# Norms in steps, a first norm by tokens, weight halves at the start, and gate tiles made while the pooling is awaited

## The chip, the cores and the metric

The kernel runs on one core of one Trainium2 chip. Its engines each have their own instruction stream: PE (TensorE, matrix products, with its weight loads PEld), DVE (VectorE), ACT (ScalarE), POOL (GpSimd) and SP (SyncE), which here issues the transfers from memory. They wait for each other by semaphores. The metric is the device time of one execution in microseconds (us); less is better.

## The reference

The kernel computes a network of two layers over 256 latent tokens and 256 context tokens (together 512 columns, the two "streams"), model width 1024. What is computed, cut to what matters:

```python
for l in range(DEPTH):                       # DEPTH = 2
    mod = (silu(c) @ w_ada[l] + b_ada[l])    # 9 vectors of 1024: shifts, scales, gates; one set per stream
    h  = ffn_half_step(h, ...)               # h + 0.5 * gate * ((silu(u @ w1) * (u @ w3)) @ w2)
    hc = ffn_half_step(hc, ...)              #   with u = rmsnorm(h) * g * (1 + scale) + shift
    y, yc = token_mixer(u, uc, ...)          # u, uc: normed and modulated again
    h = h + mod[:, :, 5] * y
    h = ffn_half_step(h, ...)                # second half step; context too, but not in the last layer

def token_mixer(u, uc, ...):
    cq, ckv, kr, pz, gq, gk, gv, ga, gr, gates = split_cols(u @ w_in)
    o_a = blocked_attend(q, k_all, v_all)    # 8 heads; low-rank q, k, v with norms and rotary
    o_p = multiscale_pool(pz, w_pool, pool_scale)
    og  = gla_bidir(qg, kg, vg, log_a, s_f, s_b)    # gated linear attention, two scans, chunks of 64
    o_g = rmsnorm(og) * silu(gr)
    g = sigmoid(gates)                       # three gates of 1024 columns
    m = g[0] * (o_a @ w_branch[0]) + g[1] * (o_p @ w_branch[1]) + g[2] * (o_g @ w_branch[2])
    return m @ w_out
```

All of it is in float32 accuracy.

## The kernel before, in words

**Products.** Activations lie with features on the partitions, tokens in the columns. A weight tile is loaded as `raw`, split by ACT into a rounded part `whi` (line 185) and by DVE into the rest `wlo = raw - whi` (`split`, line 197). An activation is split in the same way (`uhi`/`ulo`, `hi`/`lo`). `mm3` (lines 215 to 221) makes one product of three matmuls: hi·whi (L219), lo·whi (L220), hi·wlo (L221). Nearly all of PE's time is such triples.

**Weights and slots.** `Weights.run_ahead` (line 94) issues loads in the order of use while fewer than RAWS = 4 raw tiles are held, and splits them while the number of held parts stays under `room`. All SBUF tiles of 128x512 come from one pool of NSLOT = 71 slots (`slot`), given out in the order in which the program asks.

**Order of the work.** The program is written out by Python; each engine runs its instructions in the order in which a scheduler puts them, near the order of the text. Two helpers mix work into places where PE would wait: `ada` makes the modulation vectors in units (`adas(n)` advances them, DVE multiplies into `adaacc`, line 358, or PE makes them with `ada` matmuls, line 327), and `filler` (line 750) makes the mixer's later column tiles.

**Start** (`setup`, line 234; `setup_rest`, line 291). SP issues the first weight tile, the eight tiles of x and context, then the `ada` tiles of column groups j = 0, 2 (sixteen of 256 KB), three more raw tiles, groups 1 and 3. PE transposes x (line 283) into `h`; the squares and their sum `acc` (`square`, lines 440 to 448) go over features, so `ms` (line 464, a product of `acc` with a constant that sums over the partitions) and `rstd` are ready only after all of `h`. Then `am`, the scale vectors, and the first norm's `ut` (471), `uhi` and `ulo` (475). `dense_first` (line 520) takes units of both w1 and w3 over the full contraction, in parts by stream.

**A norm** (`norm`, line 455) is a generator that makes both streams' `ms`, `rstd`, `uhi` and `ulo` in one step, when the next stage begins. `grow` (line 493) adds a finished tile to `h` (line 501), squares it and adds it to `acc` (line 448). A stage ends with the second stream of its last tiles; PE then makes `ms` for both streams. The transitions stand, by the profile's time, at 422 (feed-forward to mixer), 899 (mixer to feed-forward), 1277 (feed-forward to feed-forward of the next layer), 1646 (feed-forward to mixer) and 1949 (mixer to the last feed-forward, one stream).

**Mixer** (`mixer`, line 665). Attention (`attend`, line 866) and the linear attention (`gla`, line 1133) are generators that yield the name of a step; after each, the pooling branch advances by one and `FILL[l][name]` credits are added; one credit advances the filler by half a column tile (12 matmuls). The filler makes the tiles of the pooling, then, in `while len(self.op) < 4: yield 1`, does nothing until the pooling is ready, then the pooling's branch with its gates, four output gates `gr`, the attention's branch, and the linear attention's branch. Steps that the prediction speaks of: `kms`, sums of squared keys (line 932); `qsum` and `rq`, the same of the queries (988, 1017); `sc`, `p`, `pt`, `pT`, `av`: scores, their exponents, transposes, copies and values (1031 to 1067); `logit`, `la`, `ket`, `A`, `ds`, `st`, `o`, `orstd`, `ot` of the linear attention (1157 to 1264), which runs two scan directions; in layer 1 first a pair for the context, then one for the latents.

## Time and profile before

| | |
|---|---|
| three runs | 2153.69, 2155.99, 2154.8 us; median 2154.8 |
| the profiled run | 2152.27 us, its span 2150.5 us |
| granted clock, mean | 0.983 |
| PE, DVE, ACT busy | 97%, 68%, 41% of the span |
| data moved | 290.43 MB, mean 135 GB/s |

A row of the timeline gives start, length, engine, line, operation, `out<-in`, sizes and a count; in brackets stands how long the engine stood idle before it, and whose end released it. A row of waits gives who waited for whom: total, times, longest. In a window's row stand busy us and counts of PE, PEld, DVE, ACT and POOL, then the granted PE clock as a share of full speed, the share of DMA engines in use and GB/s. The clock is at full or at half speed; a mean between these says for how much of the window it was half.

### The profile page before, as it was taken

The page shows a single profiled execution, that of the slowest core. Times are in us where ns is not written, and L with a number is a line of the kernel's source. Part 1 is how long each engine was busy: PE and PEld are TensorE (multiplying, and loading weights), DVE is VectorE, ACT ScalarE, POOL GpSimd, SP SyncE. Part 2 cuts the span into 40 slices and gives each one's busy share as a digit, 9 for nine tenths or more (in the row PEclk, how much of TensorE's full clock was granted, in tenths as well). Part 3 has the DMA queues.
Part 4 walks back from the last instruction along what each step waited for, and adds up shares of the span by engine and source line. Part 5 has one row for each costly group of instructions (what it writes and reads, how often), then busy time and mean ns, then how long its engine had stood idle before and what let it go on. Part 6 is the DMA issues. An engine that isn't in the chain of part 4 may idle for free.

```text
span 2150.5 us, 29894 instructions
## 1 busy us (share of the span) xinstructions
PE 2084.2 (97%) x11388; PEld 1752.5 (81%) x11388; DVE 1453.7 (68%) x2870; ACT 882.3 (41%) x1797; POOL 2.0 (0%) x10
## 2 busy tenths in 40 slices
PE   7999999898999999999999989999999998999999
PEld 4888778786777887888888888888888777998997
DVE  4577877867586665666876785767544687666564
ACT  5232223455344555433223342323343656665552
POOL 0000000000000000000000000000000000000000
PEclk9999999999999999999999999999999989999999
DMA  9355554514432223445555453546442332566663
GB/s 318 100 152 157 172 166 134 160 39 127 118 108 69 79 69 98 119 124 152 164 164 161 135 149 102 151 141 186 137 115 59 96 101 80 142 163 192 181 197 127
DMA packets 431071, 290.43 MB, mean 135 GB/s; under 512 B 16464, under 2 KB 386768, under 8 KB 430928
## 3 DMA queue, kind: packets, MB, share of 16 engines
q1 hardware_dynamic: 430016, 287.09, 46.6%
q8 instruction: 89, 1.46, 0.3%
q10 hardware_dynamic: 912, 1.44, 0.2%
q14 instruction: 54, 0.44, 0.1%
HBM read 287.44 MB, written 1.05 MB: 134 GB/s over the span
## 4 chain that ended last, share of the span: by engine, by line
PE 74%; DVE 11%; DMA 9%; ACT 3%; issue 2%; ACTq 0%; SPq 0%; DVEq 0%
PE ps L219 17%; PE ps L220 17%; PE ps L221 17%; DMA raw<-in_ffn_w_dram 9%; PE fill L219 4%; PE fill L221 4%; PE fill L220 4%; DVE wlo L197 4%; DVE adaacc L358 2%; ACT whi L185 2%; PE sc L1031 1%; PE av L1067 1%; PE ada L327 1%; PE pt L1049 1%; PE gv L219 1%
## 5 line engine op out<-in xcount | busy, mean ns | idle before, releaser
L197 DVE TENSOR_TENSOR wlo<-raw,whi 128x512 fp32r<-128x512 f32 (+3 forms) x912 | 531.3, 619 | 290.0 <-ACT whi L185 279.6
L185 ACT ACTIVATE whi<-raw 128x512 fp32r<-128x512 f32 (+3 forms) x912 | 471.9, 568 | 521.5 <-DMA raw<-in_ffn_w_dram 469.8
L219 PE MATMUL ps<-uhi,whi 128*128 128x512 f32 (+1 forms) x1620 | 564.3, 350 | 8.7 <-ACT uhi L185 5.1
L221 PE MATMUL ps<-uhi,wlo 128*128 128x512 f32 (+1 forms) x1620 | 561.8, 348 | 1.1 <-DVE wlo L197 1.1
L220 PE MATMUL ps<-ulo,whi 128*128 128x512 f32 (+1 forms) x1620 | 562.3, 348 | 0.0
L219 PEld LDWEIGHTS ps<-uhi,whi 128*128 128x128 f32 x1620 | 308.0, 191 | 53.7 <-ACT uhi L185 8.7
L221 PEld LDWEIGHTS ps<-uhi,wlo 128*128 128x128 f32 x1620 | 308.8, 191 | 41.3 <-DVE wlo L197 3.6
L220 PEld LDWEIGHTS ps<-ulo,whi 128*128 128x128 f32 x1620 | 309.3, 191 | 37.9 <-DVE ulo L475 0.6
L358 DVE SCALAR_TENSOR_TENSOR adaacc<-raw,csil,adaacc 128x512 f32<-128x512 f32 x420 | 294.6, 744 | 1.6 <-DMA raw<-in_w_ada_dram 0.8
L219 PE MATMUL ps<-hi,whi 128*128 128x512 f32 (+1 forms) x738 | 272.8, 371 | 6.9 <-DVE h L501 5.4
L221 PE MATMUL ps<-hi,wlo 128*128 128x512 f32 (+1 forms) x738 | 272.0, 369 | 0.2 <-DVE wlo L197 0.2
L220 PE MATMUL ps<-lo,whi 128*128 128x512 f32 (+1 forms) x738 | 271.5, 368 | 0.0
L219 PE MATMUL fill<-uhi,whi 128*128 128x512 f32 (+1 forms) x576 | 203.9, 354 | 0.0
L221 PE MATMUL fill<-uhi,wlo 128*128 128x512 f32 (+1 forms) x576 | 195.9, 340 | 0.0
L220 PE MATMUL fill<-ulo,whi 128*128 128x512 f32 (+1 forms) x576 | 195.4, 339 | 0.0
L219 PEld LDWEIGHTS ps<-hi,whi 128*128 128x128 f32 x738 | 141.2, 191 | 29.8 <-DVE h L501 5.8
L221 PEld LDWEIGHTS ps<-hi,wlo 128*128 128x128 f32 x738 | 141.2, 191 | 23.2 <-DVE wlo L197 0.6
L220 PEld LDWEIGHTS ps<-lo,whi 128*128 128x128 f32 x738 | 141.3, 192 | 22.4 <-DVE lo L197 0.2
L570 DVE TENSOR_TENSOR silu<-silu,ps 128x512 f32<-128x512 f32 (+1 forms) x88 | 54.2, 616 | 133.7 <-ACT silu L185 79.3
L185 ACT ACTIVATE silu<-ps 128x512 f32<-128x512 f32 (+1 forms) x88 | 47.4, 539 | 195.4 <-PE ps L221 195.1
L219 PEld LDWEIGHTS fill<-uhi,whi 128*128 128x128 f32 x576 | 109.3, 190 | 21.7 <-issue 10.6
L220 PEld LDWEIGHTS fill<-ulo,whi 128*128 128x128 f32 x576 | 109.4, 190 | 13.5 <-issue 2.4
(265 smaller groups left out, 2192.0 us busy)
## 6 DMA issues: line engine op xcount, KB each, us to landing
raw<-in_ffn_w_dram SPq DMA_DIRECT2D x198, 512.0 KB, 4.4
raw<-in_w_ada_dram SPq DMA_DIRECT2D x128, 512.0 KB, 3.8
raw<-in_w_in_dram SPq DMA_DIRECT2D x86, 512.0 KB, 4.4
...
raw<-in_w_branch_dram SPq DMA_DIRECT2D x48, 256.0 KB, 2.9
ada<-in_w_ada_dram SPq DMA_DIRECT2D x32, 256.0 KB, 5.4
...
```

The source lines that it names most:

```text
L185: i = self.nc.scalar.activation(**k)
L197: self.nc.vector.tensor_tensor(out=lo, in0=src, in1=f32hi, op=ALU.subtract)
L219: mm(out, wh, xh, start=start, stop=False)
L220: mm(out, wh, xl, start=False, stop=False)
L221: mm(out, wl, xh, start=False, stop=stop)
L327: nc.tensor.matmul(ps[32 * g:32 * g + 32, :], self.csil[:, k, :], r[i], start=(k < 4), stop=(k >= 4))
L358: nc.vector.scalar_tensor_tensor(out=acc[s], in0=r[i], scalar=c, in1=acc[s], op0=ALU.mult, op1=ALU.add)
L570: nc.vector.tensor_tensor(out=s[:, 0:n], in0=s[:, 0:n], in1=p3[:, 0:n], op=ALU.mult)
L1031: nc.tensor.matmul(sc[:, 0:nk], q[h][:, tt * P:(tt + 1) * P], keys[h][:, k0:T], start=True, stop=True)
L1049: nc.tensor.transpose(pt[:, (2 * x + j) * P:(2 * x + j + 1) * P], ps_[j][:, (kt + x) * P:(kt + x + 1) * P], self.ident)
L1067: nc.tensor.matmul(av[0][64 * x:64 * x + 64, s * NL:(s + 1) * NL], v[2 * s + kt][:, (h + x) * 64:(h + x) * 64 + 64], pts[x][kt // 2][:, (k ...
```

## The change

- **Start.** x is loaded first, the first raw tiles behind the first `ada` groups, and at most three ahead of group 1. ACT squares x by tokens (`xsq`, summing along the row), DVE multiplies x by the token's factor into `xr`, PE transposes `xr` (32 transposes) into `hr`, besides the residual (32 as before, 16 now behind the first `ada` group). `first_norm` makes `uhi` on ACT from `hr` by scale and bias. `both` loads halves of the contraction, of w1 and w3 together; `dense_first` goes over half of the contraction for all six outputs, then over the other. `wlo` of the first tiles is put behind `ulo` (`seconds`). `setup_rest`'s loads go from ACT's queue to SP's.
- **Norms.** `norm` yields after each stream's mean. `norm_ahead` makes the first stream's mean inside the last stage, before its last 33 matmuls (before the last tile of the output product, in the mixer); `norm_go` fetches that stream's `uhi`, and the second stream's mean follows in `dense` after two steps of the first (`then`). `rstd` has a tile of its own.
- **Mixer.** While the pooling is awaited, up to GATES = (2, 12) tiles of `later` (the eight gates of the pooling's branch, then the four output gates) are made. FILL, POOL and two places of `yield` change.

The core of the diff:

```diff
-NHALF, NSLOT, ROOM_FFN, ROOM_MIX, RAWS = 4, 71, 20, 20, 4
-ROOM_0, ROOM_1, LAST = 8, 36, 4
-S0, S1, S2 = 7, 3, 3
-        dict(a0=1, a1=1.5, k=2, q=3.5, qs=0.5, s=2, t=2, g1=0.5, g2=0, g3=0.5, g4=1, g5=0.5, w=0.5))
-POOL = (0, 1)
+NHALF, NSLOT, ROOM_FFN, ROOM_MIX, RAWS = 4, 70, 20, 20, 4
+ROOM_1, ROOM_2, LAST = 16, 36, 4
...
+        dict(a0=1, a1=1.5, k=2, v=0, q=3.5, qs=1.5, s=2, t=2, g1=1.5, g2=0, g3=1, g4=1, g5=0.5, w=0.5))
+POOL = (1, 1)
+GATES = (2, 12)
...
+        second = lambda: self.nc.vector.tensor_tensor(out=lo, in0=src, in1=f32hi, op=ALU.subtract)
+        if self.net.seconds is None:
+            second()
+        else:
+            self.net.seconds.append(second)
...
+    def both(self, srcs, k0, c0):
+        views = [s[k0 * P:(k0 + 4) * P, c0:c0 + P].rearrange("(k p) c -> p k c", p=P) for s in srcs]
+        def load(t):
+            return [self.nc.sync.dma_start(out=t[:, i * T:(i + 1) * T].rearrange("p (k c) -> p k c", k=4), in_=v)
+                    for i, v in enumerate(views)]
+        return self.w.get(load, 2 * T, lambda r, hi, lo: self.halves(r, hi, lo, 2 * T))
...
+                self.w.run_ahead(3)
...
+        sums, fac = self.tiny(8, "xsum"), self.tiny(8, "xfac")
+        junk = self.slot(name="xsq")
+        xr = []
+        for j in range(4):
+            for c in range(2):
+                self.act(out=junk, in_=xin[j][c], func=AF.Square, accum_out=sums[:, 2 * j + c:2 * j + c + 1])
+            f = fac[:, j:j + 1]
+            nc.vector.tensor_tensor(out=f, in0=sums[:, 2 * j:2 * j + 1], in1=sums[:, 2 * j + 1:2 * j + 2], op=ALU.add)
+            self.act(out=f, in_=f, func=AF.Ln, scale=1.0 / D, bias=self.eps[:, 0:1])
+            self.act(out=f, in_=f, func=AF.Exp, scale=-0.5)
+            xr.append([self.slot(name="xr") for _ in range(2)])
+            for c in range(2):
+                normed = nc.vector.tensor_scalar(out=xr[j][c], in0=xin[j][c], scalar1=f, scalar2=None, op0=ALU.mult)
+        self.xin = xin
+        self.residual(range(4), [normed])
+        self.hr = []
         for k in range(KD):
-            ps = self.ps()
-            for j in range(4):
-                nc.tensor.transpose(ps[:, j * P:(j + 1) * P], xin[j][k // 4][:, (k % 4) * P:(k % 4 + 1) * P], self.ident)
+            t = self.slot(name="hr")
             if k % 2:
-                self.act(out=self.h[:, k, :], in_=ps, func=AF.Copy)
+                self.act(out=t, in_=self.turned(xr, k), func=AF.Copy)
             else:
-                nc.vector.tensor_copy(self.h[:, k, :], ps)
-            for s in range(2):
-                self.square(k, s)
+                nc.vector.tensor_copy(t, self.turned(xr, k))
+            self.hr.append(t)
...
-            i = nc.scalar.dma_start(out=to, in_=src)
+            i = nc.sync.dma_start(out=to, in_=src)
             if self.tc:
-                self.behind(i, self.users[-1:])
+                self.behind(i, [self.last])
...
-        if l == 0 and i == 0:
-            for c in streams:
-                mean(c)
+        for s, c in enumerate(streams):
+            mean(c)
             yield u
-            for parts in (([0], range(1, 4)), (range(4, KD),)):
-                for ks in parts:
-                    for s, c in enumerate(streams):
-                        some(s, c, ks)
-                yield
-        else:
-            for s, c in enumerate(streams):
-                mean(c)
-                some(s, c, range(KD))
+            some(s, c, range(KD))
             yield u
+    def norm_ahead(self, l, i):
+        order = [(l, i) for l in range(DEPTH) for i in (0, 3, 6)]
+        self.ahead = self.norm(*order[order.index((l, i)) + 1], T)
+        next(self.ahead)
+    def norm_go(self, l, i, n):
+        norm = self.ahead
+        if norm is None:
+            norm = self.norm(l, i, n)
+            next(norm)
+        self.ahead = None
+        u = next(norm)
+        return u, lambda: [next(norm) for _ in range(2)] if n == T else None
+    def first_norm(self):
+        nc = self.nc
+        u = []
+        for ks in ([0], [1], [2, 3], range(4, KD)):
+            for k in ks:
+                assert {(0, 0, k // 4), (0, 1, k // 4)} <= self.have
+                hi, lo = self.slot(F32R, "uhi"), self.slot(F32R, "ulo")
+                u.append((hi, lo))
+                for s in range(2):
+                    c = slice(s * NL, (s + 1) * NL)
+                    t, a, b = self.half("ut"), self.am[0][1][:, k, s:s + 1], self.mod[0][:, k, s:s + 1]
+                    self.act(out=hi[:, c], in_=self.hr[k][:, c], func=AF.Identity, scale=a, bias=b)
+                    nc.vector.tensor_scalar(out=t, in0=self.hr[k][:, c], scalar1=a, scalar2=b, op0=ALU.mult, op1=ALU.add)
+                    nc.vector.tensor_tensor(out=lo[:, c], in0=t, in1=hi[:, c].bitcast(F32), op=ALU.subtract)
+            yield u
+        self.hr = None
...
-    def dense(self, units, x, n, by_stream=False):
+    def dense(self, units, x, n, by_stream=False, then=None):
         out = [self.ps() for _ in units]
         n = n if isinstance(n, list) else [n] * len(units)
                     c = slice(s * NL, (s + 1) * NL) if by_stream else slice(0, m)
                     if c.stop <= m:
                         self.mm3(o[:, c], unit.block(k), (x[k][0][:, c], x[k][1][:, c]), k == 0, k == nk - 1)
+                if then and s == 0 and k == 1:
+                    then()
...
+        out = [self.ps() for _ in range(6)]
+        for half, groups in ((0, (range(4), range(4, 6))), (1, (range(6),))):
             for g in groups:
-                for cs, ks in ((both, [0]), (streams, [1, 2, 3])) if k0 == 0 else ((streams, [4, 5, 6]), (both, [7])):
-                    for c in cs:
-                        for k in ks:
-                            for j in g:
-                                self.mm3(out[j][:, c], units[j].block(k), (x[k][0][:, c], x[k][1][:, c]), k == 0, k == KD - 1)
-                            if then:
-                                then.pop(0)()
-        self.w.done(*units)
+                for k in range(4 * half, 4 * half + 4):
+                    for j in g:
+                        self.mm3(out[j], units[half][j // 2].block(j % 2 * 4 + k % 4), x[k], k == 0, k == KD - 1)
+                    if then:
+                        then.pop(0)()
+            self.w.done(*units[half])
...
-            u = next(norm)
+            self.residual(range(4, KD))
+            self.xin = None
             self.adas(5)
-            self.w.room = ROOM_0
-            first = unit(0)
+            part = lambda half, ms: [self.both((w1, w3), 4 * half, m * P) for m in ms]
+            first = [], []
+            for m in (0, 1):
+                self.seconds = []
+                self.w.room = 4 * m + 4
+                first[0].extend(part(0, [m]))
+                u = next(norm)
+                for second in self.seconds:
+                    second()
+            self.seconds = None
             next(norm)
             self.w.room = ROOM_1
-            first += unit(1) + unit(2)
+            first[0].extend(part(0, [2]))
+            first[1].extend(part(1, [0]))
+            def rest():
+                self.adas(1)
+                next(norm)
+                self.w.room = ROOM_2
+                first[1].extend(part(1, [1, 2]))
...
+                    if c.start and k == 6:
+                        self.norm_ahead(l, i)
...
+        def out_last(dcs):
+            us = [self.cols(a["w_out"][l], 0, KD, dc * P) for dc in dcs]
+            o = [self.ps() for _ in us]
+            for c in (slice(0, NL), slice(NL, T)):
+                for dc, unit, p in zip(dcs, us, o):
+                    for k in range(KD):
+                        self.mm3(p[:, c], unit.block(k), (m[k][0][:, c], m[k][1][:, c]), k == 0, k == KD - 1)
+                    if c.start and dc == dcs[0]:
+                        self.norm_ahead(l, 3)
                     self.grow(p, dc, l, 5, c, True)
+            self.w.done(*us)
...
+        later = [gate(8 + j) for j in range(8)] + [out_gate(g) for g in range(4)]
+        spare = GATES[l]
         while len(self.op) < 4:
-            yield 1
+            if spare:
+                spare -= 1
+                yield from later.pop(0)
+            else:
+                yield 1
...
+        yield "v"
         key_tail(*pend)
+        yield "v"
...
-            yield "g1"
+        yield "g1"
+        yield "g1"
```

PE at the transition at 422, before. `ps<-hi,..` is the end of the feed-forward, `ms` the means, `vrow` a small transpose, `uhi`, `ulo` the mixer's first products:

```order
L221 MATMUL ps<-hi,wlo 128x256
L691 MATMUL ps<-cst_72,vrow 128x128
L464 MATMUL ms<-acc,cst_72 128x256 x2
L219 MATMUL ps<-uhi,whi 128x256 x4
L220 MATMUL ps<-ulo,whi 128x256
```

After (33 matmuls from the first mean to the end of the feed-forward):

```order
L239 MATMUL ps<-hi,wlo 128x256
L514 MATMUL ms<-acc,cst_72 128x256
L237 MATMUL ps<-hi,whi 128x256
L238 MATMUL ps<-lo,whi 128x256
...
L239 MATMUL ps<-hi,wlo 128x256
L788 MATMUL ps<-cst_72,vrow 128x128
L237 MATMUL ps<-uhi,whi 128x256 x4
L514 MATMUL ms<-acc,cst_72 128x256
L238 MATMUL ps<-ulo,whi 128x256
```

The first mean has moved ahead of the last 33 matmuls; the second stands behind the first four of the mixer. The same holds at 1277 and 1646; at 899, 24 matmuls stand ahead of the second mean.

PE at the end of mixer 0's query tiles, before; 24 fill matmuls stand between `qsum` and `rq`:

```order
L221 MATMUL pool<-hi,wlo 128x512
L988 MATMUL qsum<-sqq,cst 32x512 x4
L219 MATMUL fill<-uhi,whi 128x512
...
L221 MATMUL fill<-uhi,wlo 128x512
L1017 MATMUL rq<-cst_72,rq 128x128 x4
```

After:

```order
L239 MATMUL q<-hi,wlo 128x512
L1108 MATMUL qsum<-sqq,cst 32x512 x4
L1137 MATMUL rq<-cst_72,rq 128x128 x4
L237 MATMUL pool<-hi,whi 128x512
L238 MATMUL pool<-lo,whi 128x512
```

`rq` now follows `qsum` with nothing between; four half gate tiles stand earlier, around `v`, `kms` and `q`.

PE in mixer 1 behind the second `ket`, before; each "..." stands for fill matmuls, 24 in all at each:

```order
L1049 MATMUL pt<-cst_72,p 128x128 x8
L1067 MATMUL av<-pT,v 64x256 x8
L219 MATMUL fill<-uhi,whi 128x256
...
L221 MATMUL fill<-uhi,wlo 128x256
L1207 MATMUL A<-qt,kt 128x128 x8
L1031 MATMUL sc<-k,q 128x512 x2
...
L1225 MATMUL ds<-gv,ket 64x128 x28
```

After, with nothing left out:

```order
L239 MATMUL fill<-uhi,wlo 128x256
L1187 MATMUL av<-pT,v 64x256 x8
L1328 MATMUL A<-qt,kt 128x128 x8
L1151 MATMUL sc<-k,q 128x512 x2
L1346 MATMUL ds<-gv,ket 64x128 x28
L1169 MATMUL pt<-cst_72,p 128x128 x8
L1365 MATMUL o<-gv,Asum 128x128 x2
L1369 MATMUL o<-st,qt 64x128
```

The fills that stood between these steps have moved ahead of the second `ket`, to the first pair's steps and the wait for the pooling; the four last score items and the whole second pair follow each other with 3 and 5 fill matmuls in two places.

86 lines of the change are left out of this document (52 added, 34 removed).

## The prediction

> **What bounds the kernel now.** I read the page first, then PE's own waits, the timeline at each of them, and the busy time by windows.
>
> ```profile
> span 2150.5 us, 29894 instructions
> PE 2084.2 (97%) x11388; PEld 1752.5 (81%) x11388; DVE 1453.7 (68%) x2870; ACT 882.3 (41%) x1797; POOL 2.0 (0%) x10
> ```
>
> PE is busy for 97% of the span: 2150.5 − 2084.2 = 66.3 us are idle, and that, with whatever PE loses at a reduced clock, is all that a new order of the same matmuls can win. Who ended the idle time:
>
> ```profile
> PE ms L464 <- DVE acc L448: 14.8, 7, 4.3
> PE ket L1186 <- DVE la L1175: 8.3, 2, 8.1
> PE ps L219 <- DVE h L501: 5.4, 2, 3.4
> PE ps L219 <- ACT uhi L185: 5.1, 3, 4.0
> PE pool L219 <- ACT hi L185: 3.8, 1, 3.8
> ```
>
> (Total us, times, longest.) Five entries hold 14.8 + 8.3 + 5.4 + 5.1 + 3.8 = 37.4 us: norms (`ms`, `uhi`, `h`), the mixer of layer 0 (`pool`) and that of layer 1 (`ket`). The change reaches all of them but `h`: the vector work in front of those two waits keeps its place, so I count nothing for them.
>
> The profiled run took 2152.27 us, span 2150.5; 1.8 us lie outside. It is 2.5 below the median 2154.8. I sum against the span and carry the difference over to the median. About 0.2% (4.3 us) is what a measurement here tells from no change.
>
> **Startup.** Rows of the load queue, of DVE and of PE (start, length, idle time ahead in brackets), and one window (busy us of each engine, then the granted clock, DMA share and GB/s):
>
> ```profile
> 6.76 10.57 SPq L255 DMA_DIRECT2D ada<-in_w_ada_dram  x16
> 6.74 5.52 PE L283 MATMUL ps<-cst,x 128*128 128x128 f32 x32
> 23.33 3.32 PE L327 MATMUL ada<-ada,csil 128*32 128x512 f32 x16
> 27.42 0.66 PE L339 MATMUL ada<-cst,adaev 128*128 128x128 f32 x4 [0.78 <-ACT adaev L185]
> 28.52 0.18 DVE L341 TENSOR_REDUCE mod<-ada 128x8 f32<-128x32 f32 x1
> 32.05 0.79 PE L219 MATMUL ps<-uhi,whi 128*128 128x512 f32 x1 [3.98 <-ACT uhi L185]
> 52.67 1.92 PE L327 MATMUL ada<-ada,csil 128*32 128x512 f32 x16
> ada<-in_w_ada_dram SPq DMA_DIRECT2D x32, 256.0 KB, 5.4
> 6.50:12.30 5.80, 5.74 (x33) 5.26 (x33) 1.29 (x3) 2.40 (x4) 0.00 (x0) 1.00 1.02 380
> ```
>
> The sixteen loads hold two groups of `ada`. The last is issued at 6.76 + 10.57 x 15/16 = 16.7 and lands 5.4 later, at 22.1. Without the 512 KB tile of weights that stood ahead of x, at 380 GB/s, all of it moves up by 1.4 us, to 20.7. If the loads decide, the second group ends at about 22.
>
> PE has more to do now. The last x is there at about 12.26 − 1.4 = 10.9 (before, the 32 transposes ended at 6.74 + 5.52, paced by the loads). Square, factor and `xr` of that last tile take an estimated 2 us, four steps of about half a microsecond: 12.9. Then come 32 transposes of `xr` (new; 5.52 at most), the first `ada` group (1.92 to 3.32), four transposes (0.66) with 16 residual ones behind (a half of 5.52 at most), and the second group (1.92 to 3.32): 24 to 28 without any overlap of copies. I take 25.
>
> From the second group's end to the first real matmul it was 32.05 − 26.65 = 5.4 us. After: the copy 0.78, four transposes 0.66, three small vector steps of 0.18, and one `uhi`, taken at 0.5 (between the small step and the four transposes): 2.5, with hand-overs 3. `rstd`'s multiplication is gone, and the four `wlo` that stood between the small steps go behind. First matmul at 25 + 3 = 28, 4 us sooner (22 + 3 = 25 to 28 + 3 = 31). The second half of the contraction needs its own `uhi` and `ulo`, and `whi` splits queued behind these on ACT; the bound below is nothing, above one landing less its cover, 3; I take 1.5. **Net 2.5 us (−1 to 6).** Cover: the weight tiles load while this runs; if they come late, the first matmul waits for them instead.
>
> A rule speaks against this part. The granted clock is 1.00 in the window at 6.50, filled by nothing but transposes. The Trainium skill, "TensorE: Matmul & The Clock Gate", Part 4, says that transposes do not count as busy for the clock gate. By that rule the added ones would leave both `ada` groups at half speed, 2 x (3.32 − 1.92) = 2.8 us, and the net gain would be gone; the row disagrees, and I keep 2.5.
>
> **Norms in steps.** The four transitions that have two streams (start, length, and idle ahead):
>
> ```profile
> 422.56 0.67 PE L464 MATMUL ms<-acc,cst 128*128 128x256 f32 x2 [1.09 <-DVE acc L448]
> 424.19 0.74 PE L219 MATMUL ps<-uhi,whi 128*128 128x256 f32 x4 [0.96 <-ACT uhi L185]
> 898.93 0.67 PE L464 MATMUL ms<-acc,cst 128*128 128x256 f32 x2 [2.15 <-DVE acc L448]
> 900.53 3.30 PE L327 MATMUL ada<-raw,csil 128*32 128x512 f32 x16
> 1277.16 1.19 PE L464 MATMUL ms<-acc,cst 128*128 128x256 f32 x2 [4.32 <-DVE acc L448]
> 1646.04 0.67 PE L464 MATMUL ms<-acc,cst 128*128 128x256 f32 x2 [1.42 <-DVE acc L448]
> 1646.89 0.74 PE L219 MATMUL ps<-uhi,whi 128*128 128x256 f32 x4 [0.17 <-ACT uhi L185]
> 1275.15 0.48 DVE L501 SCALAR_TENSOR_TENSOR h<-ps,am,h 128x256 f32<-128x256 f32 x1
> ```
>
> The first stream's mean now stands 33 matmuls before the end of the stage. Four matmuls of this width take 0.74 us at 1646.89, so that is 4 us or more, and by the end the first `uhi` is ready. But the second mean, at 422, 1277 and 1646, stands behind only four matmuls of the next stage, and waits for the same last `h`, its square and its sum as both means did. So what goes is what the four matmuls cover, and the second half of the way (mean, `rstd`, `uhi`), not the wait for the sum: at 422 the first real matmul came 424.19 − 421.47 = 2.7 us after PE ran dry (422.56 − 1.09), and I leave 1.5, **1.2**; at 1646 it came 2.3 after, and I leave 1.0, **1.3**; at 1277 the last `h` comes only at 1275.15 out of a backlog on DVE whose order is kept, and of 4.32 I take off **1.0**. At 899 24 matmuls stand between, over 4 us, and the mean should wait for nothing: 2.15 idle, and the `ada` group at 1.92 instead of 3.30 (1.38), **3.5**. Sum **7.0**: 3 if each second mean waits longer, because the sum now stands behind a first `ut` on DVE (0.48 each, as `h`), 9 if all idle time but that at 1277 goes. The norm at 1949 has one stream and stays.
>
> **Mixer 0.**
>
> ```profile
> 486.27 1.12 PE L932 MATMUL kms<-sqk,cst 128*128 128x512 f32 x2 [2.40 <-DVE k L938]
> 488.18 0.79 PE L219 MATMUL q<-hi,whi 128*128 128x512 f32 x1 [0.78 <-ACT sqk L185]
> 499.17 0.80 PE L219 MATMUL pool<-hi,whi 128*128 128x512 f32 x1 [3.78 <-ACT hi L185]
> 484.00:506.00 22.00, 15.17 (x45) 10.54 (x49) 18.07 (x30) 10.04 (x20) 0.00 (x0) 0.77 0.34 95
> 513.43 0.68 ACT L185 ACTIVATE rq<-qsum,eps 128x512 f32<-128x512 f32 x1
> 514.52 0.72 ACT L185 ACTIVATE rq<-rq,eps 128x512 f32<-128x512 f32 x1
> ```
>
> Idle: 2.40 + 0.78 + 3.78 = 6.96. The window's clock of 0.77 means 22 x 0.23 / 0.5 = 10.1 us at half speed; what that costs lies between (10.1 − 6.96) / 2 = 1.6 and 5.0, and I take 4.0, because the matmuls right behind both gaps are slow. So 11.0 are to be had. Two gate tiles in four halves (48 matmuls of full width; over 9 us even by the mean of all matmuls, 2084.2 / 11388 = 0.18) now stand around these places and cover them. But the 24 matmuls between the last `qsum` and the `rq` transposes are gone. PE waits there for the last square, then for what ACT has queued: a `hi`, Ln 0.68, a `whi` split, Exp 0.72. At 0.6 each for the other three that is 3.2, with hand-overs 3.7 idle, and 2.3 lost to the clock, a little over half of the 4.0 above, since a gap of this size stood there too. **Net 11 − 6 − 1 (small waits at `q`) = 4** (0 to 9).
>
> **Mixer 1.**
>
> ```profile
> 1746.49 0.71 PE L1244 MATMUL o<-gv,Asum 128*128 128x128 f32 x4 [1.67 <-DVE op L1128]
> 1774.44 1.13 PE L1157 MATMUL logit<-ga,wa 32*128 32x512 f32 x4
> 1750.83 0.58 PE L219 MATMUL pool<-hilo,whi 128*128 128x256 f32 x1 [1.84 <-ACT hilo L185]
> 1794.02 1.11 PE L1186 MATMUL ket<-cst,la 128*128 128x128 f32 x4 [8.09 <-DVE la L1175]
> 1744.00:1762.00 18.00, 12.94 (x59) 7.82 (x58) 14.66 (x44) 5.54 (x16) 0.00 (x0) 0.62 0.15 44
> 1786.00:1800.00 14.00, 5.98 (x31) 4.36 (x32) 9.60 (x21) 9.42 (x19) 0.00 (x0) 0.63 0.26 75
> 1762.00:1786.00 24.00, 23.94 (x176) 20.88 (x174) 19.51 (x42) 18.23 (x38) 0.00 (x0) 1.00 0.43 111
> L181 ACT ACT_TABLE_LOAD x26 | 33.4, 1283 | 2.3 <-issue 1.8
> 1812.15 1.88 DVE L1233 SCALAR_TENSOR_TENSOR st<-st,dec,ds 128x128 f32<-128x128 f32 x6
> ```
>
> The windows at 1744 and 1786 hold 5.06 + 8.02 = 13.1 idle, and by their clocks 18 x 0.38 / 0.5 = 13.7 and 14 x 0.37 / 0.5 = 10.4 us at half speed; by the same two bounds the clock costs 4.3 to 6.8 and 1.2 to 5.2, of which I take 5.1 and, since the second window's slow time is mostly the idle time itself, 2.2. So 20.4 are to be had.
>
> Up to twelve tiles of 256 columns are made ahead here (24 matmuls each), and in the new order fills stand between all steps of the first pair (`A`, `ds`, `o`, `ot`): the first window's 5.06 + 5.1 = 10.2 go. At the second `ket`, 93 fill matmuls, one `pt` and one `sc` follow the `logit`; at 0.136 each (176 in 23.94 us) that is 12.6, with the two steps about 14. They face a chain that took 1794.02 − 1775.57 = 18.5, with table loads and gate steps inside it; without two loads of 1.28, 15.9, without the gate steps some 13. So 2 of these 10.2 stay (0 to 5).
>
> But the fills are spent by then. From that `ket` on, attention and the second pair stand almost bare (8 fill matmuls in all), where 24 lay between any two steps. There the chain decides: `ds`, 14 steps of `st` at 0.31 (row 1812.15), with the `p` steps of DVE mixed between, and `o`: 4.4 + 3 = about 8 us, against some 5 of `pt`, `sc` and `o` on PE: 3 idle; `orstd` and the last `pT` add 1 each: 5 idle, 1 of clock. The end below is 1.5 (PE has enough short steps to turn to), the end above 9 (twice the chain's excess, all of it cold). **Net 20.4 − 2 − 6 = 12.4, say 12.5** (4 to 18).
>
> A rule on what short gaps cost: the gaps of the first window are 1.67 and 1.84 and less, and it still ran at 0.62. The Trainium skill, same page, section "Why this matters for your kernels", asks only for no idle gaps over about 3 us. By that the 5.1 would not come from these gaps, nor would the bare end lose clock: 12.5 − 5.1 + 1 ≈ 8. The windows speak against it.
>
> **Sum:** 2.5 + 7 + 4 + 12.5 = 26. 2152.27 − 26 = 2126; carried to the median, 2154.8 − 26 ≈ **2129**.
>
> **The rivals.** (1) The forecast, near 2129: 0.61. (2) *The bare end eats mixer 1's gain.* In the chain of `sc`, maximum, exponent, product, transposes, copy, `av`, each of the five items there exposes 2 us more than I charge: −10, time 2139. For it: nothing lies between them in the new order; against it: items overlap two by two. 0.14. (3) *Norms and startup give next to nothing*, since the second means wait as both did before and the transposes delay `ada`: 26 − 8, time 2137. For it: four matmuls are little cover; against it: the first `uhi` no longer waits. 0.08. (4) *The short gaps did not cost the clock*, which runs slow there for another reason: mixer 1 gives 8 and the time is 2133. The rule of the Trainium skill above would have it so; the windows at 1744 and 1762 (0.62 with gaps, 1.00 without) do not. 0.05. (5) *More than I think:* the second `ket` and the `rq` stall are covered, and the bare end too: 2115 to 2119. 0.06. (6) *Slower: slots.* Up to twelve tiles, half a slot each, wait in slots for their branch, and there is one slot fewer; splits of weights then wait for a free one, and PE for each unit. Twelve units that each wait one landing, 5.4 us for 256 KB as the first rows have it, would cost 65 us; from 26 / 12 = 2.2 us a unit on the change loses. At 3 us: −26 + 36 = +10, 2165. Against it: weights hardly end a PE wait today (row below, 3.5 us in all). 0.06.
>
> ```profile
> PE ps L219 <- ACT whi L185: 3.5, 3, 2.0
> ```
>
> **How the numbers follow.** The terms' ranges, not all bad or good at once, give 26 ± 13; that is 2116 to 2142. Reaching to the lower end of rival 5 and past rivals 2 and 3, **2112 to 2148** leaves out rival 6 (0.06), the worst of rivals 2 and 3 (0.07) and a little below (0.03). Faster by over 0.2%: cases 1 to 5 (0.94) without the worst of 2 and 3 together, 0.89; within 0.2%: 0.06; slower: rival 6, of which the light end is within, 0.05.
>
> **What would show it.** PE idle falls from 66 to about 47, the clock is 1.00 around 486 and 1746; `ms` waits total 5 to 8; a new wait `rq` of 3 to 4 and waits of `o`, `ot` or `pt` in mixer 1's end of 3 to 7; the first real matmul at about 28. I am wrong if `whi` waits appear by the dozen, if the bare end idles over 10 us, or if the first matmul comes at 31 or later.

## The result and the profile after

| | before | changed |
|---|---|---|
| median, range | 2155.14 us, 2153.69 to 2155.99 | 2126.89 us, 2124.41 to 2130.35 |
| the profiled run, its span | 2152.27, 2150.5 us | 2130.35, 2128.2 us |
| PE idle in the span | 66.3 us | 58.8 us |
| granted clock, mean | 0.983 | 0.991 |

Four runs of each give a ratio of 0.9871 (95% interval 0.9854 to 0.9888): 28 us or 1.3% faster, against 26 predicted (2129.0, range 2112 to 2148). The profiled run is the slowest of its four, so its span shows 22.3 of the 28 us. One of the five executions of u_mix1b (below) took 8004 us and is left out of its ratio.

The head of the page, after:

```profile
span 2128.2 us, 29785 instructions
PE 2069.4 (97%) x11308; PEld 1740.4 (82%) x11308; DVE 1450.9 (68%) x2872; ACT 888.0 (42%) x1805; POOL 2.0 (0%) x10
```

PE's idle time fell by 66.3 − 58.8 = 7.5 us, and its busy time by 14.8 us. The products are the same; at the start some are merely made in wider pieces. What fell is the time at half speed: by the mean clocks from 2150.5 x 0.017 x 2 = 73 us to 2128.2 x 0.009 x 2 = 38, and each of these 35 us costs up to half of itself. So the gain came less from waits than the prediction had it, and more from the clock. PE's waits after (total us, times, longest), those that answer to the list of before:

```profile
PE ps L237 <- ACT uhi L189: 9.2, 4, 4.3
...
PE ms L514 <- DVE acc L498: 4.5, 3, 3.0
PE fill L237 <- ACT whi L189: 4.0, 1, 4.0
...
PE rq L1137 <- ACT rq L189: 3.2, 1, 3.2
...
PE ot L1385 <- DVE mx L1155: 1.8, 1, 1.8
...
PE o L1369 <- DVE st L1354: 1.2, 1, 1.2
```

`ms` went from 14.8 to 4.5, `ket <- la` (8.3) and `pool <- hi` (3.8) are gone. In their place stand longer waits for `uhi` (5.1 before, 9.2 now), the new `rq` and, not foreseen, one `fill` that waits 4.0 for a weight split.

**The ledger by stage.** Each stage is cut at the same instruction in every kernel, and its length compared with that of before; idle time and clock come from the windows between these cuts. "Half" is the time at half speed, (1 − clock) x 2 x length. The traces hold no clock record before the first time the clock goes to full (at 10.1 us before, 9.5 after, up to 20.5 in other runs), and the column counts the time ahead of it as 1.00; so "half" of the start is too low. All from one profiled run each:

| stage (before's time) | length, before → after | idle | half |
|---|---|---|---|
| start to first `silu` (0 to 72) | 72.2 → 69.7 | 15.0 → 13.4 | 11 → 14 |
| first feed-forward (72 to 355) | 282.9 → 283.2 | 4.6 → 3.6 | 2 → 2 |
| norm at 422 (355 to 453) | 97.6 → 96.0 | 5.7 → 6.2 | 6 → 4 |
| mixer 0 to its `sc` (453 to 578) | 124.8 → 119.2 | 7.0 → 3.9 | 11 → 4 |
| norm at 899 (693 to 926) | 233.2 → 228.6 | 4.3 → 1.5 | 5 → 0 |
| norm at 1277 (1207 to 1303) | 95.7 → 96.0 | 6.3 → 8.7 | 10 → 8 |
| norm at 1646 (1583 to 1669) | 86.4 → 85.9 | 1.6 → 1.5 | 0 → 0 |
| mixer 1 and the norm at 1949 (1669 to 1965) | 295.7 → 287.5 | 16.1 → 14.0 | 30 → 6 |

The two mixers' windows, before and after, show it without the table (busy us of PE, PEld, DVE, ACT and POOL, then clock, DMA share, GB/s):

```profile
452.80:577.60 124.80, 117.84 (x504) 92.10 (x504) 85.51 (x160) 57.53 (x120) 0.00 (x0) 0.96 0.37 105
1669.00:1964.70 295.70, 279.63 (x2078) 244.62 (x2078) 212.53 (x464) 179.23 (x392) 0.00 (x0) 0.95 0.47 127
```

```profile
448.90:568.10 119.20, 115.29 (x504) 90.31 (x504) 85.70 (x159) 58.26 (x120) 0.00 (x0) 0.99 0.40 110
1654.80:1942.40 287.60, 273.61 (x2078) 241.00 (x2078) 210.68 (x464) 179.55 (x393) 0.00 (x0) 0.99 0.48 131
```

The same number of matmuls (504, 2078) takes 2.6 and 6.0 us less of busy time: that is clock. The last stage lost only 16.07 − 13.99 = 2.1 us of idle time.

### The profile page after: what moved, and what is told of

Read it like the earlier page. It is cut to its first block, busy times and chain, and to the rows that moved or that the text cites. A ratio compares the mean times of both kernels' runs of the same rounds, so it can differ in the third digit from the quotient of the medians.

```text
span 2128.2 us, 29785 instructions
## 1 busy us (share of the span) xinstructions
PE 2069.4 (97%) x11308; PEld 1740.4 (82%) x11308; DVE 1450.9 (68%) x2872; ACT 888.0 (42%) x1805; POOL 2.0 (0%) x10
## 4 chain that ended last, share of the span: by engine, by line
PE 75%; DVE 10%; DMA 9%; ACT 4%; issue 2%; ACTq 0%; DVEq 0%; SPq 0%
PE ps L237 18%; PE ps L239 17%; PE ps L238 17%; DMA raw<-in_ffn_w_dram 8%; PE fill L237 4%; PE fill L239 4%; PE fill L238 4%; DVE wlo L201 4%; DVE adaacc L408 2%; ACT whi L189 2%; PE sc L1151 1%; PE av L1187 1%; PE gv L237 1%; PE pt L1169 1%; PE gv L239 1%
## 5 line engine op out<-in xcount | busy, mean ns | idle before, releaser
L201 DVE TENSOR_TENSOR wlo<-raw,whi 128x512 fp32r<-128x512 f32 (+4 forms) x912 | 531.8, 618 | 277.9 <-ACT whi L189 269.4
L189 ACT ACTIVATE whi<-raw 128x512 fp32r<-128x512 f32 (+4 forms) x912 | 472.5, 568 | 523.9 <-DMA raw<-in_ffn_w_dram 473.1
L237 PE MATMUL ps<-uhi,whi 128*128 128x512 f32 (+1 forms) x1584 | 556.9, 354 | 12.0 <-ACT uhi L189 9.2
L238 PE MATMUL ps<-ulo,whi 128*128 128x512 f32 (+1 forms) x1584 | 555.9, 351 | 0.0
L239 PE MATMUL ps<-uhi,wlo 128*128 128x512 f32 (+1 forms) x1584 | 555.0, 351 | 0.7 <-DVE wlo L201 0.7
L237 PEld LDWEIGHTS ps<-uhi,whi 128*128 128x128 f32 x1584 | 300.1, 190 | 57.1 <-ACT uhi L189 11.7
L239 PEld LDWEIGHTS ps<-uhi,wlo 128*128 128x128 f32 x1584 | 301.1, 190 | 42.8 <-DVE wlo L201 3.6
L238 PEld LDWEIGHTS ps<-ulo,whi 128*128 128x128 f32 x1584 | 301.5, 190 | 39.1 <-DVE ulo L566 0.4
L239 PEld LDWEIGHTS fill<-uhi,wlo 128*128 128x128 f32 x576 | 110.1, 191 | 13.6 <-issue 0.6
```

What stands on the lines that cost most here:

```text
L189: i = self.nc.scalar.activation(**k)
L201: second = lambda: self.nc.vector.tensor_tensor(out=lo, in0=src, in1=f32hi, op=ALU.subtract)
L237: mm(out, wh, xh, start=start, stop=False)
L238: mm(out, wh, xl, start=False, stop=False)
L239: mm(out, wl, xh, start=False, stop=stop)
```

## The experiments

Their own runs of before differ by up to 7.5 us from one set of runs to the next, so the ratio and the ledger are compared, not the time. The first four undo one part each; they shared the runs of before (2148.72 us, 11 runs).

**u_start: the start as before.** setup, the first norm, `dense_first` and the ROOM numbers as before, all else as changed:

```diff
-            norm = self.first_norm()
+            norm = self.norm(l, i, n)
...
-        out = [self.ps() for _ in range(6)]
-        for half, groups in ((0, (range(4), range(4, 6))), (1, (range(6),))):
+        out = [self.ps() for _ in units]
...
+        for k0, groups in ((0, (range(4), range(4, 6))), (4, (range(6),))):
```

> The changed kernel with the start as before (features-wise norm, full contraction, rests of the loads on ACT's queue); norms in steps and the mixers as changed. The profiles of before and after, set side by side, give the start 2.3 us of the gain (first real matmul 1.3 sooner, the rest in the second half of the contraction). Theory: 2.3 slower than the changed kernel, first real matmul at about 32.0. Rival (the start gives next to nothing, since DVE's residual copies and the transposes delay ada): within 1 us of the changed kernel. My prediction's term was 2.5.

2126.89 us, ratio 0.9904 (0.9889 to 0.9919). The first real matmul comes at 32.1 and the first `silu` at 72.4, as before (32.0, 72.2), against 30.7 and 69.7 in the changed kernel. The start is worth about 2.5 us there; in further profiles of the same start (below) 2.5 to 5.6.

**u_norm: no mean ahead.**

```diff
-        self.ahead = self.norm(*order[order.index((l, i)) + 1], T)
-        next(self.ahead)
+        return
...
-        return u, lambda: [next(norm) for _ in range(2)] if n == T else None
+        if n == T:
+            for _ in range(2):
+                next(norm)
+        return u, None
```

> The changed kernel with no mean made ahead: both streams' means, and both uhi, at the start of the next stage, as before. Profiles side by side give the norms 6 us: 1.6 at 422, 3.0 at 899, 0.7 at 1277, 0.7 at 1646. Theory: 6 us slower than the changed kernel, the waits of ms for acc back to some 10 us in all. Rival (norms give next to nothing): within 2 us. Prediction's term: 7.

2127.24 us, ratio 0.9902 (0.9889 to 0.9916). PE's waits for the norms in it:

```profile
PE ms L514 <- DVE acc L498: 12.6, 5, 5.6
...
PE ps L237 <- ACT uhi L189: 2.9, 3, 1.8
```

Against 4.5 and 9.2 after: what the norms in steps take from `ms` (8.1) they give back to `uhi` for the most part (6.3). The ledger of the four norms: 0.0, −3.3, 0.0 and +1.5 against before, where the changed kernel has −1.6, −4.6, +0.3 and −0.5. So at 899 only 1.3 of 4.6 us are the mean's; the rest stays without it. There `ms` waits 1.42 in u_norm instead of 2.15 before, and no half speed follows; whether the new order of the last output tiles does that was not tried apart.

**u_mix0: mixer 0 as before.** `GATES` (0, 12), the old `FILL[0]`, `POOL[0]` 0, no yields at "v" in layer 0.

```diff
-FILL = (dict(a0=1.5, a1=2, k=1.5, v=1, q=0.5, qs=2, s=0.5, t=1, g1=3, g2=3.5, g3=1.5, g4=1.5, g5=0, w=0.5),
+FILL = (dict(a0=1.5, a1=2, k=1.5, v=0, q=0, qs=2, s=0.5, t=1, g1=3, g2=3.5, g3=1.5, g4=1.5, g5=0, w=0.5),
...
-POOL = (1, 1)
-GATES = (2, 12)
+POOL = (0, 1)
+GATES = (0, 12)
```

> The changed kernel with layer 0's mixer as before (no gate tiles ahead, no fills at v, POOL and FILL of layer 0 as before). Profiles side by side give mixer 0 5.5 to 6 us. Theory: 5.5 slower than the changed kernel; waits kms 2.4 and pool 3.8 back, the wait rq of 3.2 gone. Rival (the new rq stall eats most): within 2 us. Prediction's term: 4.

2126.63 us, ratio 0.99 (0.9886 to 0.9913). The waits return and `rq` is gone:

```profile
PE pool L237 <- ACT hi L189: 3.6, 1, 3.6
PE kms L1050 <- DVE k L1056: 2.4, 1, 2.4
```

The stage is 1.3 us shorter than before, against 5.6 after.

**u_mix1: mixer 1 without its gate tiles and fills**, its yields at "g1" inside the loop over directions as before, but with the new yields at "v":

```diff
-        dict(a0=1, a1=1.5, k=2, v=0, q=3.5, qs=1.5, s=2, t=2, g1=1.5, g2=0, g3=1, g4=1, g5=0.5, w=0.5))
+        dict(a0=1, a1=1.5, k=2, v=0, q=3.5, qs=0.5, s=2, t=2, g1=0.5, g2=0, g3=0.5, g4=1, g5=0.5, w=0.5))
...
-GATES = (2, 12)
+GATES = (2, 0)
```

> The changed kernel with layer 1's mixer as before (no tiles ahead, old FILL, a g1 after each direction). Profiles side by side give mixer 1 8.6 us in the profiled run. Theory: 8.6 slower than the changed kernel; ket wait of 8 back, the wait fill for whi of 4.0 gone. Rival (the whole term of my prediction is there and the profiled run of the changed kernel was a slow one of its kind): 12 or more slower. Second rival (the bare end eats the gain): within 3 us.

2138.95 us, ratio 0.9953 (0.9939 to 0.9967). The waits of before return (and one of 2.4 of `ds` for `op`):

```profile
PE ket L1310 <- DVE la L1295: 7.4, 1, 7.4
...
PE pool L237 <- ACT hilo L189: 5.0, 2, 3.4
```

The stage is 6.2 us longer than before: the two yields alone, with nothing to fill them, do harm. That called for **u_mix1b**, which has mixer 1 wholly as before, those yields too (in a later set, before 2147.67 us, 8 runs):

```diff
+        if not l:
+            yield "v"
         key_tail(*pend)
-        yield "v"
+        if not l:
+            yield "v"
```

> The changed kernel with layer 1's mixer wholly as before: no tiles ahead, old FILL, a g1 after each direction, and no yields at v in layer 1 either. The first undoing kept those two yields, each of which also advances the pooling by a step, and its mixer came out 6 us longer than before the change. Theory (the yields at v without fills to go with them did that): the stretch from mixer 1 to the last feed-forward is as long as before the change (295.7 us, within 1), and the worth of the mixer 1 part is 8 to 9 us. Rival (old mixer 1 fits worse behind the new norm and start, whatever the yields): it stays 3 to 6 longer.

2131.82 us, ratio 0.9928 (0.9907 to 0.9949). Its stage is 0.5 shorter than before, its half-speed time 24 us (30 before, 6 after), and `ket <- la` waits 8.1 again. Mixer 1's part is worth some 8 us.

The next four shared another set (before 2154.03 us, 7 runs), **again** being the changed kernel itself:

> The changed kernel itself once more, on the chip of this call, as the measure for the three others. Ratio to before 0.987 as in the first comparison, first matmul at 30 to 31, mixer 1 with the wait of fill for whi of 4.0.

2126.71 us, ratio 0.9874 (0.9859 to 0.9888). By the ledger it is 27.1 us shorter than before, where the first profile was 22.3, though the instructions are the same: start −4.2 instead of −2.5, first feed-forward −1.0 instead of +0.2, norm at 1277 −1.9 instead of +0.3, mixers −5.6 and −8.8. What varies between runs is the start, the first feed-forward and the norms at 422 and 1277, not the mixers.

**m_g1in: layer 1's two yields at "g1" inside the loop over directions**, against the wait of 4.0 for `whi`:

```diff
-        yield "g1"
-        yield "g1"
+            if l:
+                yield "g1"
+        if not l:
+            yield "g1"
+            yield "g1"
```

> The changed kernel, but in layer 1 the linear attention yields after each of its two directions again, instead of twice after both. In the changed kernel a fill matmul waits 4.0 us at 1718.8 for whi, and ACT's row shows that split queued behind the second direction's exponent, which waits for DVE's scan, while its raw tile landed some 10 us before. Theory (a weight split stands in ACT's in-order queue behind the gates' chain): with the first yield between the directions, the split is queued ahead of the second direction and the 4.0 wait goes; mixer 1 gets 3 to 4 us shorter. Rival (slots or the load hold the split back): the wait stays at 3 to 5. Second rival (the fill only moves): the wait goes, but ket or the bare end waits that much longer, no change.

2123.72 us, ratio 0.9861 (0.9847 to 0.9876). The `fill` waits fall to 1.9, and one that was gone returns:

```profile
PE ket L1310 <- DVE la L1295: 3.3, 1, 3.3
...
PE fill L237 <- ACT whi L189: 1.9, 2, 1.4
```

The stage is 0.9 us shorter than in **again** (9.7 against 8.8 below before), and the intervals of the two ratios overlap: the wait changed its place.

**m_res: all residual transposes behind the first `ada` group.**

```diff
-        self.residual(range(4), [normed])
...
-            self.residual(range(4, KD))
+            self.residual(range(KD))
```

> The changed kernel with all residual transposes and copies behind the first ada group instead of half of them ahead of it. In the changed kernel DVE copies four residual tiles (16.8 to 19.2) ahead of its four hr tiles (19.2 to 21.6), and PE's transposes of xr wait for those buffers. Theory (DVE's copies set the start): first ada group 1.5 to 2.5 us sooner, first real matmul at 28 to 29 instead of 30.7. Rival (the loads of the second ada group decide, the last is issued at 16.3 and lands 5.4 later): second group not before 21.7 + 0.6, which also allows 28; if the clock or loads bind, the first matmul stays at 30 or later.

2128.24 us, ratio 0.9878 (0.9862 to 0.9895). Freed of the residual's copies, the start is no sooner: the first real matmul comes at 30.4 (in **again**, of the same set, at 29.8).

```profile
12.76 5.74 PE L325 MATMUL ps<-cst,xr 128*128 128x128 f32 x32 [5.65 <-DVE xr L310]
18.42 1.92 PE L373 MATMUL ada<-ada,csil 128*32 128x512 f32 x16
...
25.22 1.92 PE L373 MATMUL ada<-ada,csil 128*32 128x512 f32 x16
```

The first `ada` group moved from 20.48 to 18.42, and the transposes that had stood ahead of it moved behind it: the second group comes at 25.22 instead of 25.53. My reason for this run, that DVE's copies set the start, falls: they held back the first `ada` group, but not the second, because the transposes of `xr` begin at the same time (12.76 against 12.64), and from there PE has transposes and `ada` groups one behind the other.

**m_ahead: the first stream's first two `uhi` made with its mean**, inside the last stage:

```diff
-            some(s, c, range(KD))
+            if s == 0 and n == T:
+                some(s, c, range(AHEAD))
+                yield u
+                some(s, c, range(AHEAD, KD))
+            else:
+                some(s, c, range(KD))
```

> The changed kernel with the first stream's first two tiles of ut, uhi and ulo made ahead together with its mean, before the last h of the stage. In the changed kernel PE waits 1.5 to 1.6 at 420 and 1632 and 4.3 at 1264 for the first uhi, whose ut stands on DVE behind the last h though rstd was ready 1.5 to 3 us before. Theory (the order on DVE behind the last h sets what is left of these waits): the uhi waits at 420 and 1632 fall below 0.6 and that at 1264 by 1 to 3, in all 3 to 5 us. My prediction's reason (the second mean waits for the last sum): the uhi waits are not the limit, ms takes their place, under 1 us in all.

2135.77 us, ratio 0.9918 (0.9903 to 0.9933): 9 us slower than the changed kernel, and my theory, that the wait for `uhi` is to be had so, falls: the waits for `uhi` shrink from 9.2 to 6.6 in all, but waits for `ulo` (2.3) and `wlo` (2.8, 0.9 after) come in their place. PE at the norm at 1646 in it:

```profile
1637.00 0.39 PE L240 MATMUL ps<-uhi,wlo 128*128 128x256 f32 x1 [0.84 <-DVE wlo L202]
...
1638.61 0.74 PE L238 MATMUL ps<-uhi,whi 128*128 128x256 f32 x4 [0.88 <-ACT uhi L190]
1639.99 0.58 PE L239 MATMUL ps<-ulo,whi 128*128 128x256 f32 x1 [0.64 <-DVE ulo L528]
```

The one gap of 1.51 that the changed kernel has here is gone, but three smaller waits, for splits of weights and of activations, come in its place. SP issues the load of `w_ukv` at 1636.01, where the changed kernel has it at 1603.02. The stages at 1277 and 1646 are 1.9 and 3.6 us longer than before. So the weights come later; the tiles taken early may take slots from them, as in rival 6 on a small scale, or the splits may stand behind others in ACT's queue. The two were not tried apart.

Three on the fills. **m_gates8** sets `GATES` to (2, 8), and **m_rq** takes layer 0's credits at "q" (with u_mix1b, before 2147.67 us):

```diff
-GATES = (2, 12)
+GATES = (2, 8)
```

> The changed kernel with 8 instead of 12 tiles ahead in layer 1, so that the four output gates (96 matmuls, 11.5 us) are made behind the pooling's branch again. Theory (the bare end costs only the some 5 us of its waits, and fills ahead of it are needed where they stand): the fills return partly to the end, waits of ot, o, av and ket there fall from some 5 to 2, and others of the same size come up ahead, within 2 us of the changed kernel. Rival from my prediction (the bare end is the dearest part): 3 or more us faster.

2123.21 us, ratio 0.9884 (0.9862 to 0.9906). It proved no change: its instructions stand in the same order as the changed kernel's, since at most eight tiles are ever made ahead (the prediction reckoned with up to twelve). So it is a third profile of the same kernel: 28.5 us shorter than before, mixers −5.6 and −8.1.

```diff
-FILL = (dict(a0=1.5, a1=2, k=1.5, v=1, q=0.5, qs=2, s=0.5, t=1, g1=3, g2=3.5, g3=1.5, g4=1.5, g5=0, w=0.5),
+FILL = (dict(a0=1.5, a1=2, k=1.5, v=1, q=0, qs=2, s=0.5, t=1, g1=3, g2=3.5, g3=1.5, g4=1.5, g5=0, w=0.5),
```

> The changed kernel with no credit for a q in layer 0, which puts 12 fill matmuls (2.8 us) between the last qsum and the rq transposes. Theory (the rq wait of 3.2 is a chain with no cover, behind it nothing else): the wait falls to below 0.8, and with the half speed behind it, layer 0's mixer gets 3 to 4 us shorter. Rival (the 12 matmuls are missed where they stood): a new wait at q of 2 to 3, no change.

2123.3 us, ratio 0.9882 (0.9864 to 0.9901). PE around the queries in it, and a window there:

```profile
501.23 1.05 PE L1108 MATMUL qsum<-sqq,cst 128*32 128x512 f32 x2
502.21 0.50 PE L238 MATMUL fill<-ulo,whi 128*128 128x512 f32 x1
...
506.79 0.66 PE L1137 MATMUL rq<-cst,rq 128*128 128x128 f32 x4 [1.30 <-ACT rq L189]
```

```profile
500.00:515.00 15.00, 13.70 (x56) 8.81 (x53) 8.48 (x15) 9.06 (x15) 0.00 (x0) 1.00 0.24 65
```

And after, the same two:

```profile
500.98 1.07 PE L1108 MATMUL qsum<-sqq,cst 128*32 128x512 f32 x8
501.97 0.50 PE L237 MATMUL pool<-hi,whi 128*128 128x512 f32 x1
...
510.59 0.66 PE L1137 MATMUL rq<-cst,rq 128*128 128x128 f32 x4 [3.18 <-ACT rq L189]
```

```profile
505.00:520.00 15.00, 11.82 (x48) 8.16 (x48) 11.28 (x20) 9.60 (x16) 0.00 (x0) 0.89 0.56 165
```

The wait fell from 3.18 to 1.30 and the clock stayed at 1.00, as hoped. But the stage is 4.9 shorter than before instead of 5.6, because the scheduler strewed the `qsum` among the fills: two records there take 502.21 − 501.23 = 0.98 us, as much as eight in a block (501.97 − 500.98 = 0.99). There are sixteen records in both kernels; they stand in six places in this run and in two blocks in the changed kernel.

Last, **m_gates4**, `GATES` (2, 4), which does leave fills for the second pair (before 2154.45 us, 7 runs):

```diff
-GATES = (2, 12)
+GATES = (2, 4)
```

> At most 4 tiles of gates instead of 12 are made while the pooling of layer 1 is awaited; the rest is made where it stood before, so that fills are left for the linear attention's second pair. Theory (the tiles are the cover of the pooling wait): PE runs out of fills before the pooling is ready; waits on op, pool or rq of 3 to 6 us come back around the steps of the first pair, the clock there falls below 1.00, and the stage of mixer 1 (8.2 us shorter than before in the changed kernel) is only 3 to 6 shorter. Rival (the bare end is the price of too many tiles): the waits of o, ot and pT at the end (4.3 us) fall under 2 and nothing returns in their place; the stage is 9.5 to 10.5 shorter. A third case: both, the waits only change places, and the stage is 7 to 9 shorter.

2138.29 us, ratio 0.9931 (0.9904 to 0.9958). One wait and two windows of PE in mixer 1:

```profile
1754.21 0.58 PE L237 MATMUL pool<-hilo,whi 128*128 128x256 f32 x1 [3.58 <-ACT hilo L189]
```

```profile
1725.00:1760.00 35.00, 27.43 (x228) 22.67 (x227) 24.49 (x67) 18.95 (x43) 0.00 (x0) 0.85 0.40 109
1800.00:1832.00 32.00, 32.00 (x274) 24.43 (x274) 25.97 (x67) 17.77 (x44) 0.00 (x0) 1.00 0.20 58
```

And after, in two windows that hold the same steps, the first pair with the pooling and the end from the second `ket` on:

```profile
1725.00:1790.00 65.00, 64.32 (x553) 57.51 (x552) 51.98 (x126) 45.88 (x99) 0.00 (x0) 1.00 0.53 141
1790.00:1832.00 42.00, 37.71 (x302) 25.73 (x302) 34.49 (x89) 25.82 (x63) 0.00 (x0) 1.00 0.09 26
```

Both theories were half right, and the first decides. The end is covered (32.00 busy of 32; one wait of 2.51 stands ahead of it, at 1792.81), but the pooling is bare again: 7.57 us idle at a clock of 0.85 in 35 us, where the changed kernel has 0.68 at 1.00. The stage is 1.7 us longer than before, 9.9 longer than after. With four of the eight tiles gone (and the credits of the changed kernel kept), all of the mixer's gain is gone; the bare end is the cheaper price.

## Why the prediction was right, point by point

Against the one profile of before, the three profiles of the changed kernel are 22.3, 27.1 and 28.5 us shorter. By terms:

| term | predicted | after, again, m_gates8 (ledger) | undone: loss by ratio |
|---|---|---|---|
| start, to the first `silu` | 2.5 (−1 to 6) | 2.5, 4.2, 3.4 | 6 |
| norms, four stages | 7.0 (3 to 9) | 6.4, 8.0, 7.1 | 6 |
| mixer 0 | 4 (0 to 9) | 5.6, 5.6, 5.6 | 5 |
| mixer 1 | 12.5 (4 to 18) | 8.2, 8.8, 8.1 | 11 |
| first feed-forward, not reckoned with | 0 | −0.2, 1.0, 4.2 | |

The last column sets each undone kernel's ratio against 0.9876, the mean of 0.9871, 0.9874 and 0.9884, times 2152 us. It is good to some 4 us, and undone parts were run on other sets than the kernel itself (u_mix1b and m_gates8 in one: 8.6 us).

- **The start: right in sum, wrong in its steps.** "I take 25", for the end of the second `ada` group, and "First matmul at 25 + 3 = 28" failed: these came at 27.45 and 30.71 (in m_gates8 at 31.10, which the prediction had named as a sign of being wrong). The last `xr` was not there at 12.9 but at 16.9: ACT squares the tiles one behind the other, from 8.94 to 15.0, and the pairs of `xr` start at 12.1, 13.7 and (the last two) 15.2. The 32 transposes waited 0.65 and 0.44 us for them, ran 0.21 us apart for the most part, which is half speed, and ended at 20.5 instead of 12.9 + 5.52 = 18.4. The way behind the second group took 3.3 instead of 3, because the first matmul spans both streams, as it did before, and waits for two `uhi` (1.09 us), where the sum has one at 0.5. Rows of PE, and of DVE for the last `xr`:

```profile
12.64 0.90 PE L326 MATMUL ps<-cst,xr 128*128 128x128 f32 x4 [2.10 <-DVE xr L310]
...
15.20 1.67 DVE L310 TENSOR_SCALAR xr<-x,xfac 128x512 f32<-128x512 f32 x4
...
20.48 1.92 PE L374 MATMUL ada<-ada,csil 128*32 128x512 f32 x16
...
25.53 1.92 PE L374 MATMUL ada<-ada,csil 128*32 128x512 f32 x16
...
30.71 1.22 PE L237 MATMUL ps<-uhi,whi 128*128 128x512 f32 x2 [1.81 <-ACT uhi L189]
```

  The first matmul came 1.3 sooner than before, not 4; but where 1.5 were then taken off for the second half of the contraction, the way to the first `silu` became 1.2 shorter (40.2 to 39.0), and the sum came out.

  The rule of the Trainium skill weighed here ("TensorE: Matmul & The Clock Gate", Part 4, transposes do not count for the gate) does not hold in these traces, but the row that the prediction held against it was misread. Its window from 6.50 shows a clock of 1.00 because the trace has no clock record before 10.06. What shows the clock is the distance of the transposes: before, they start 0.21 us apart up to 10.1 and 0.11 apart behind it (so they were not "paced by the loads" either). In m_res, where nothing but transposes runs ahead of the first record at 16.60, the distance falls from 0.21 to 0.11 there. Two windows of m_res, both with PE busy throughout and the clock column at 1.00, hold six and eleven of them:

```profile
13.00:14.00 1.00, 1.00 (x6) 0.90 (x5) 0.43 (x3) 1.00 (x5) 0.00 (x0) 1.00 1.04 383
...
17.00:18.00 1.00, 1.00 (x11) 1.00 (x10) 0.78 (x2) 0.92 (x3) 0.00 (x0) 1.00 1.05 385
```

  So transposes alone brought the clock up, both `ada` groups ran at 1.92, and the loss of 2.8 that I drew from the rule did not come.

- **The norms: the size right, the reason wrong.** The step that failed is that the second mean "waits for the same last `h`, its square and its sum as both means did". It waits for nothing (420.49); what is late is the first `uhi` of the first stream:

```profile
419.91 0.74 PE L237 MATMUL ps<-uhi,whi 128*128 128x256 f32 x4 [1.60 <-ACT uhi L189]
420.49 0.59 PE L514 MATMUL ms<-acc,cst 128*128 128x256 f32 x2
```

```profile
416.56 0.42 ACT L189 ACTIVATE rstd<-rstd 128x256 f32<-128x256 f32 x1
...
418.24 0.48 DVE L578 SCALAR_TENSOR_TENSOR h<-ps,am,h 128x256 f32<-128x256 f32 x1 [0.50 <-PE ps L239]
...
418.84 0.47 DVE L523 SCALAR_TENSOR_TENSOR ut<-h,am,rstd 128x256 f32<-128x256 f32 x1
```

  `rstd` is ready at 416.98, but the first `ut` stands on DVE behind the other stream's last `h`, which cannot start before PE has finished at 418.2. So "by the end the first `uhi` is ready" was wrong as well. At 1277 the same order costs 4.32 (`uhi` at 1264.42) where `ms` waited 4.32 before: no gain, 1.0 predicted (in **again** the wait is 3.29 and the gain 1.9). At 899 the mean waits for nothing and the clock holds, as said: 4.6 against 3.5, though by u_norm only 1.3 of it from the mean.

- **Mixer 0: right**, with a new `rq` wait of 3.18 (3.7 predicted) and 4 us at half speed left of 11. (The 48 matmuls of cover come to 8.8 us by the mean that the prediction takes, not to over 9; nothing hangs on it.)

- **Mixer 1: the mis-sized step is "the first window's 5.06 + 5.1 = 10.2 go".** The clock was won as reckoned: 6.0 us of busy time, where 5.1 + 2.2 − 1 = 6.3 were charged. But idle time of the stage fell by 2.1 (3.9 in again), not by 13.1 − 2 − 5 = 6.1. Of the missing 4.0, some 2.1 lie behind the mixer, at the norm at 1949: `ms` waits 3.02 there (2.73 before), and two groups of `ada` matmuls wait 0.45 and 1.34 for their weights, which they do not in again and m_gates8. In the mixer itself idle time fell by 4.2, from 13.35 to 9.15. What no term had is one wait of 3.96. With fills between the steps, PE reaches the weights of these fills sooner, and one split stands on ACT's queue behind the gates' chain, which itself waits for DVE. Its load had gone out at 1690.36 and landed 3.9 us later, some 24 us before the split began (not some 10, as I wrote ahead of m_g1in). The rows of PE at the two places, of ACT and of SP:

```profile
1718.80 0.39 PE L237 MATMUL fill<-uhi,whi 128*128 128x256 f32 x1 [3.96 <-ACT whi L189]
...
1930.66 1.05 PE L374 MATMUL ada<-raw,csil 128*32 128x512 f32 x4 [1.34 <-DMA raw<-in_w_ada_dram]
```

```profile
1717.29 0.63 ACT L189 ACTIVATE e<-b 128x512 f32<-128x512 f32 x1 [2.15 <-DVE b L1291]
...
1718.13 0.61 ACT L189 ACTIVATE whi<-raw 128x512 fp32r<-128x512 f32 x1
```

```profile
1690.36 0.37 SPq L219 DMA_DIRECT2D raw<-in_w_in_dram  x1
```

  That the mixer did not fall further behind is because its end cost less than predicted. The second `ket` waits 0.54 + 0.52 (2 predicted), and the bare end behind it 0.32 + 1.16 + 1.75 = 3.2 (5 predicted), together the 42.00 − 37.71 = 4.29 of the window at 1790, where 7 were charged. Its clock was 1.00, so the 1 us charged there was not lost, and rival 2 did not come. The Trainium skill's section "Why this matters for your kernels" (the same page), which asks only for no gaps over about 3 us, agrees with these gaps of 1.16 and 1.75.

- **"PE idle falls from 66 to about 47" failed** (58.8; 52.9 and 53.1 in the profiles of again and m_gates8). The gain came out nevertheless, because busy time fell by 14.8, where a good 7 were charged: at 422 and 1277 idle time even rose, by 0.5 and 2.4, but busy time fell by 2.1 at each. The size of the sum was luck in part: the norm at 899 and mixer 0 gave more than their terms, mixer 1 less.

- **Rivals.** 3 (norms and start next to nothing) falls by the ledger. 6 (slots) did not come: no `whi` waits by the dozen. 4 (short gaps cost no clock) is right for nearly all single gaps below 1.8 us (counted in the last section), but not for the window at 1744, whose half-speed time is gone with its gaps and stays in u_mix1b, where they are back.

What stays open: why the first feed-forward, the start and the norm at 1277 differ by 2 to 5 us between runs of one and the same order. In the first feed-forward part of it is waits for weight splits: 0.65, 1.13 and 1.67 us (from 256 to 293) in the first profile, 1.21 and 0.68 in m_gates8.
